# The low part of six weight halves moves from VectorE to GpSimd

## The chip, the cores and the metric

The kernel runs on one core of a Trainium2 chip. The metric is the time of one execution on the device in microseconds (us); less is better. The engines are called as the profile calls them: PE is TensorE's matrix multiplication, PEld its weight loads, DVE is VectorE, ACT is ScalarE, POOL is GpSimd, SP is SyncE, whose queue issues the weight loads from memory.

## The reference

Two layers of a hybrid decoder trunk over 256 positions of width 1024, in float32. A layer is a feed-forward block, a mixer block (causal pooling and block-sparse attention in parallel, merged by gates) and a second feed-forward block. The change touches the first block of the first layer only:

```python
def rms_norm(x, g):
    xf = x.astype(jnp.float32)
    y = xf * lax.rsqrt(jnp.mean(xf * xf, axis=-1, keepdims=True) + EPS)
    return (y * g.astype(jnp.float32)).astype(x.dtype)

def swiglu(h, w_gate_up, w_down):
    a, b = jnp.split(h @ w_gate_up, 2, axis=-1)
    return (jax.nn.silu(a) * b) @ w_down

def hybrid_layer(x, ...):
    x = x + 0.5 * swiglu(rms_norm(x, ffn1_norm), ffn1_w_gate_up, ffn1_w_down)
    ...
```

The hidden width of the block is 2816, which is 22 slices of 128.

## The kernel before, in words

**Split operands.** Each float32 operand is multiplied as two parts: a high part `hi` in a rounded format that TensorE multiplies fast, and a low part `lo`, which is the operand minus its high part. For weights ACT makes the high part with a copy (line 123) and DVE the low part with a subtraction (line 124). A product takes one multiplication of the weight's high part with both parts of the activations (512 columns) and one of its low part with the activations' high part (256 columns).

**Units.** Weights come in units of 128 x 2048 numbers (1 MB), in the order of use, `NU` of them. `request` (line 98) asks for the next one: it takes a buffer for the raw unit out of four, lets SP's queue load it, and splits each half (128 x 1024) into `hi` and `lo`; these have six buffers each, which is three units of two halves. `unit` hands the oldest unit that was asked for to the multiplications.

**The first feed-forward block.** One unit holds the weights of one slice of 128 hidden channels, gate and up side by side. `pair` (line 174) multiplies a unit by the activations into a PSUM tile `ps`, asks for the next unit, and drains the tile: ACT copies the half with the correction to SBUF (line 186), DVE adds the main half (line 187). PSUM has two such tiles, so unit n+2 cannot start before the drain of unit n is through. In the profile's rows the drained tiles are called `hold` for the first eight slices and `ab` after.

**The norm's factor comes late.** The multiplications start on activations that are not normalised, and the factor `r`, one number for each position, is applied to the drained tiles. It is made in `factor_spread`: the sum of squares is put through TensorE (`ss`), then ACT takes the reciprocal root (line 303) and DVE refines it (lines 302 and 304 to 306). Units 0 to 2 are worked side by side at the start; unit 3 follows with the sum of squares in its midst. Slices that were drained before `r` is there are finished afterwards, at most two for each further unit (lines 349 to 357): DVE multiplies by `r` (353), ACT takes the SiLU (355), DVE multiplies gate by up (356), and `halves` makes the two parts of the product (202 on ACT, 203 on DVE).

**Order of work.** Every engine works through its own queue in order. TensorE's order is that of the code. DVE's, ACT's and POOL's order is set when the program is built, by a scheduler that weighs what is ready; only operations marked `keep` stay in the order of the code. POOL has no work after the first 10 us in this kernel.

Of the kernel before, what the change touches and what calls it, by code (L numbers as in the profile page):

```python
# [18 lines left out]
F32 = mybir.dt.float32  # L19
F32R = mybir.dt.float32r  # L20
AF = mybir.ActivationFunctionType
OP = mybir.AluOpType
# [16 lines left out]
HALF = 8 * P  # L39
# [11 lines left out]
def trunk_kernel(ctx: ExitStack, tc: tile.TileContext, x_in, w_in, pw_in, qkn_in, rope_in, mask_in, band_in, out):  # L51
    nc = tc.nc
# [10 lines left out]
    def quarter(name):  # L63
        return pat.tile([P, 2, S], F32, name=name, tag="at")
# [11 lines left out]
    tt = nc.vector.tensor_tensor  # L76
# [6 lines left out]
    def banks(pool, name):  # L83

        return pool.tile([P, 2, 2, S], F32, name=name, tag="mm" if pool is pmm else "at2")
# [6 lines left out]
    def unit():  # L92

        if not ahead:
            request()
        return ahead.pop(0)

    def request(then=(), put=lambda i: i):

        if n_unit[0] == NU:  # L100
            return
        raw, hi, lo = buffers()
        u = n_unit[0]
        n_unit[0] += 1
        n = HALF if u < 4 else 2 * HALF
        for c in range(0, 2 * HALF, n):
            nc.sync.dma_start(raw[:, c:c + n], w_in[u, :, c:c + n])
        for h in range(2):
            split(raw[:, h * HALF:(h + 1) * HALF], hi[h], lo[h], put)
            for t, ps in then[h:h + 1]:  # L110
                drain(t, ps, put)
                for f in range(4 + 2 * h, 6 + 2 * h):
                    square_x(f, put)
        ahead.append((hi, lo))

    def buffers():
        raw = raws.tile([P, 2 * HALF], F32, name="raw", tag="raw")
        hi = [parts.tile([P, HALF], F32R, name="hi", tag="hi") for _ in range(2)]
        lo = [parts.tile([P, HALF], F32R, name="lo", tag="lo") for _ in range(2)]
        return raw, hi, lo  # L120

    def split(w, hi, lo, put=lambda i: i):
        put(act(hi, w, AF.Copy))  # L123
        put(tt(lo, w, hi.bitcast(F32), op=OP.subtract))  # L124

    def blk(z, b, n=1):

# [13 lines left out]
    def chain(ps, hi, lo, b, xk, first, last):  # L141

        prod(ps, blk(hi, b), xk, first, False)
        return prod(ps[:, 0, :], blk(lo, b), xk[:, 0, :], False, last)

    def chain3(ps, hi, lo, b, xs, first=True, last=True):

        for i, xk in enumerate(xs):
            prod(ps, blk(hi, b + i), xk[:, 0, :], first and i == 0, False)
            prod(ps, blk(hi, b + i), xk[:, 1, :], False, False)  # L150
            prod(ps, blk(lo, b + i), xk[:, 0, :], False, last and i == len(xs) - 1)

    def columns(w, ps, ks):

        for k in ks:
            for j in range(2):
                chain(ps[j] if isinstance(ps, list) else ps[:, j], *w, 2 * k + j, hk[k], k == 0, k == NK - 1)
# [13 lines left out]
            for k, j, d in bs:  # L171
                prod(d[:, 1, :], blk(hi, 2 * k + j), hk[k][:, 1, :], False, False)

    def pair(w, t, other=None, at=0, more=True):

        ps = banks(pmm, "ps")
        columns(w, ps, range(at))
        if other:
            other()
        columns(w, ps, range(at, NK))  # L180
        if more:
            request()
        drain(t, ps)

    def drain(t, ps, put=lambda i: i):
        put(act(t, ps[:, :, 1, :], AF.Copy))
        put(tt(t, ps[:, :, 0, :], t, op=OP.add))

    def pairs(ws, ts):

        pss = [banks(pmm, "ps"), banks(pmm, "ps"), [quarter("pe") for _ in range(2)]]
        for a, b in PIECES:
            for w, ps in zip(ws, pss):
                columns_high(w, ps, range(a, b), a == 0 and w is ws[0])
        request(list(zip(ts[:2], pss)), keep)
        for j, pe in enumerate(pss[2]):
            keep(act(ts[2][:, j, :], pe[:, 1, :], AF.Copy))
            keep(tt(ts[2][:, j, :], pe[:, 0, :], ts[2][:, j, :], op=OP.add))

    def halves(d, v, put=lambda i: i):  # L200

        put(act(d[:, 0, :], v, AF.Copy))
        put(tt(d[:, 1, :], v, d[:, 0, :].bitcast(F32), op=OP.subtract))
# [41 lines left out]
    def square_x(f, put=lambda i: i):  # L245

        if f == 0:
            act(acc, x[:, f, :], AF.Square)
        else:
            sq = small.tile([P, S], F32, name="sq", tag="sq", bufs=2)  # L250
            put(act(sq, x[:, f, :], AF.Square))
            put(tt(acc, acc, sq, op=OP.add))
# [38 lines left out]
    def factor_spread(mid=lambda: None, put=lambda i: i):  # L291


        ar = small.tile([P, 2, S], F32R, name="ar", tag="dr", bufs=1)
        halves(ar, acc, put)
        r = small.tile([P, S], F32, name="r", tag="r", bufs=2)
        h, a = (small.tile([P, S], F32, name=n, tag="sq", bufs=2) for n in "ha")
        ss = quarter("ss")[:, 0]
        for j in range(2):
            prod(ss, one_r, ar[:, j, :], j == 0, j == 1)  # L300
        mid()
        put(nc.vector.tensor_scalar(h, ss, 1.0 / D, EPS, op0=OP.mult, op1=OP.add))
        put(act(r, ss, AF.Abs_reciprocal_sqrt, scale=1.0 / D, bias=eps))
        stt(a, r, -0.5, r, op0=OP.mult, op1=OP.mult)
        tt(a, a, h, op=OP.mult)
        stt(r, a, 1.5, r, op0=OP.add, op1=OP.mult)
        return r

    def bc2(a):
        return a.unsqueeze(1).to_broadcast([P, 2, a.shape[-1]])  # L310

    def ffn(after, n0=0, end=False):
        gs = []
        for n, m in (("ga", 8), ("gc", 8), ("gb", NF - 16)):
            g = acts.tile([P, m, 2, S], F32R, name=n, tag=n)
            gs.extend(g[:, i] for i in range(m))
        abs_ = []

        hold = acts.tile([P, NK, 2, S], F32, name="hold", tag="gates")

        def wide():
            i = len(abs_)
            abs_.append((i, hold[:, i] if i < NK else tmp.tile([P, 2, S], F32, name="ab", tag="t512", bufs=5)))
            return abs_[-1][1]

        r = []

        def sums(*a):
            r.append(factor_spread(*a))

        if n0:
            pairs([unit() for _ in range(n0)], [wide() for _ in range(n0)])
            pair(unit(), wide(), lambda: sums(lambda: request((), keep), keep), 6, False)
        else:
            ws = [unit() for _ in range(2)]
            ts = [wide() for _ in range(2)]
            pss = [banks(pmm, "ps") for _ in range(2)]
            for u, k0, k1 in ((0, 0, NK - 1), (1, 0, 2), (0, NK - 1, NK), (1, 2, 4)):
                columns(ws[u], pss[u], range(k0, k1))
            drain(ts[0], pss[0])  # L340
            sums()
            columns(ws[1], pss[1], range(4, NK))
            drain(ts[1], pss[1])
        done = 0
        for i in range(n0 + 1 if n0 else 2, NF + 1):
            if i < NF:
                pair(unit(), wide())

            todo = range(done, min(done + 2, i) if i < NF else NF)
            done = todo.stop  # L350
            for j in todo:
                ab = abs_[j][1]
                tt(ab, ab, bc2(r[0]), op=OP.mult)
                sg = small.tile([P, S], F32, name="sg", tag="sg", bufs=2)
                act(sg, ab[:, 0, :], AF.Silu)
                tt(sg, sg, ab[:, 1, :], op=OP.mult)
                halves(gs[j], sg)
        for b in range(NK * NF):
            f, k = divmod(b, NF)
            if b % 16 == 0:  # L360
                hi, lo = unit()
            if k == 0:
                ps = quarter("ps")
            if f < NK - 1 or not end:
                chain(ps, hi, lo, b % 16, gs[k], k == 0, k == NF - 1)
            else:
                chain3(ps[:, 0, :], hi, lo, b % 16, gs[k:k + 1], k == 0, k == NF - 1)
            if k == NF - 1:
                add_x(f, ps, f < NK - 1 or not end)
                after(f)  # L370

    def add_x(f, ps, two):
        t = x[:, f, :]
        if two:
            t = small.tile([P, S], F32, name="t", tag="sg", bufs=2)
            act(t, ps[:, 1, :], AF.Copy)
            stt(t, t, 0.5, x[:, f, :], op0=OP.mult, op1=OP.add)
        keep(stt(x[:, f, :], ps[:, 0, :], 0.5, t, op0=OP.mult, op1=OP.add))  # L378
# [108 lines left out]
    def mix(l, after):  # L487
# [19 lines left out]
        def gate(f, *other):  # L507
            pair(unit(), gates[:, f], *other)
# [312 lines left out]
```

## Time and profile before

| | |
|---|---|
| median of 3 runs | 1007.2 us (1003.53, 1007.2, 1007.35) |
| the profiled execution | 1003.93 us |
| its span, first to last instruction | 1002.1 us |
| busy: PE, DVE, ACT, POOL | 997.7, 791.6, 623.0, 5.3 us |
| granted clock of TensorE | 1.0 |
| stretch 20 to 65 us: DVE, ACT, POOL busy | 43.05, 35.08, 0.00 of 45 us |

A row of the profile names a line of the kernel, an engine, an operation, what it writes and reads (`out<-in`, without buffer numbers), shapes and the number of instructions. In rows in order of time the first two numbers are start and duration in us, and brackets tell how long the engine stood idle before and who ended that. In rows of groups the numbers after the bar are busy time in us, the mean of one in ns, and idle time before. In rows of waits they are the total in us, how often, and the longest.

### The profile page before, as it was taken

How to read it: one execution, taken by the hardware profiler on the slowest of the kernel's cores; microseconds unless marked ns; L12 is line 12 of the kernel's file. 1: busy time of each engine (PE TensorE's matmuls, PEld its weight loads, DVE VectorE, ACT ScalarE, POOL GpSimd, SP SyncE). 2: the span in 40 equal slices, each digit the busy share in tenths (PEclk: the TensorE clock that was granted, in tenths of full speed). 3: DMA queues.
4: the chain of work that ended last, by engine and by line, in shares of the span. 5: the costliest groups of instructions: out<-in, count | busy, mean ns of one | idle time of the engine just before them, and what ended most of it. 6: DMA issues, size and time to landing. Idle time of an engine off the chain costs nothing.

```text
span 1002.1 us, 16021 instructions
## 1 busy us (share of the span) xinstructions
PE 997.7 (100%) x6350; PEld 906.2 (90%) x6350; DVE 791.6 (79%) x1168; ACT 623.0 (62%) x976; POOL 5.3 (1%) x34
## 2 busy tenths in 40 slices
PE   9999999999999999999999999999999999999998
PEld 8888899898999988988889999888989999888898
DVE  7998866599878888886688888666997888888752
ACT  7866655557756766665576666556678567666541
POOL 2000000000000000000000000000000000000000
PEclk9999999999999999999999999999999999999999
DMA  9676555643536665565556566555544365565640
GB/s 313 253 248 214 186 201 202 219 170 128 210 127 210 206 214 173 206 210 191 191 187 215 182 209 206 183 201 189 185 181 167 135 214 202 190 202 196 208 149 22
DMA packets 31163, 192.91 MB, mean 192 GB/s; under 512 B 3504, under 2 KB 7344, under 8 KB 8560
## 3 DMA queue, kind: packets, MB, share of 16 engines
q1 hardware_dynamic: 30528, 190.79, 55.5%
q8 instruction: 50, 0.82, 0.3%
q0 software_dynamic: 272, 0.79, 0.3%
q10 hardware_dynamic: 288, 0.31, 0.1%
q14 instruction: 25, 0.20, 0.1%
HBM read 190.82 MB, written 1.05 MB: 191 GB/s over the span
## 4 chain that ended last, share of the span: by engine, by line
PE 100%; DVE 0%; issue 0%
PE ps L81 85%; PE pt L81 6%; PE two L81 4%; PE at L81 2%; PE pe L81 1%; PE at L470 1%; PE busy L81 0%; PE tp L432 0%; PE st L81 0%; PE ss L81 0%; DVE gx L378 0%; DVE ones L212 0%; DVE eps L220 0%
## 5 line engine op out<-in xcount | busy, mean ns | idle before, releaser
L81 PE MATMUL ps<-hx,hi 128*128 128x512 f32 (+1 forms) x1714 | 572.8, 383 | 0.0
L124 DVE TENSOR_TENSOR lo<-raw,hi 128x1024 fp32r<-128x1024 f32 (+2 forms) x372 | 439.9, 1188 | 135.1 <-ACT hi L123 127.4
L123 ACT ACTIVATE hi<-raw 128x1024 fp32r<-128x1024 f32 (+2 forms) x372 | 380.2, 1030 | 230.4 <-PE ps L81 182.6
L81 PE MATMUL ps<-hx,lo 128*128 128x256 f32 x1712 | 464.6, 273 | 0.0
L81 PEld LDWEIGHTS ps<-hx,hi 128*128 128x128 f32 x1714 | 320.9, 188 | 57.2 <-issue 0.3
L81 PEld LDWEIGHTS ps<-hx,lo 128*128 128x128 f32 x1712 | 321.2, 188 | 0.9
L81 PE MATMUL ps<-gc,hi 128*128 128x512 f32 (+1 forms) x264 | 87.0, 376 | 0.0
L81 PE MATMUL ps<-ga,hi 128*128 128x512 f32 (+1 forms) x264 | 87.0, 376 | 0.0
L81 PE MATMUL ps<-gc,lo 128*128 128x256 f32 x256 | 69.9, 273 | 0.0
L81 PE MATMUL ps<-ga,lo 128*128 128x256 f32 x256 | 69.9, 273 | 0.0
L81 PE MATMUL ps<-gb,hi 128*128 128x512 f32 (+1 forms) x198 | 65.6, 376 | 0.0
L81 PE MATMUL pt<-hi,hx 128*128 128x512 f32 x192 | 65.1, 385 | 0.0
L81 PEld LDWEIGHTS ps<-ga,hi 128*128 128x128 f32 x264 | 49.0, 188 | 8.3
L81 PEld LDWEIGHTS ps<-gc,hi 128*128 128x128 f32 x264 | 49.0, 188 | 8.3
L81 PE MATMUL pt<-lo,hx 128*128 128x256 f32 x192 | 52.6, 274 | 0.0
L81 PE MATMUL ps<-gb,lo 128*128 128x256 f32 x192 | 52.4, 273 | 0.0
L81 PEld LDWEIGHTS ps<-ga,lo 128*128 128x128 f32 x256 | 48.1, 188 | 0.0
L81 PEld LDWEIGHTS ps<-gc,lo 128*128 128x128 f32 x256 | 48.1, 188 | 0.0
L81 PE MATMUL ps<-mk,hi 128*128 128x256 f32 x256 | 44.1, 275 | 0.0
L81 PE MATMUL two<-yp,hi 128*128 128x256 f32 x256 | 44.1, 275 | 0.0
L81 PEld LDWEIGHTS ps<-gb,hi 128*128 128x128 f32 x198 | 36.7, 188 | 6.2
L81 PEld LDWEIGHTS pt<-hi,hx 128*128 128x128 f32 x192 | 36.0, 188 | 6.8
(149 smaller groups left out, 1041.4 us busy)
## 6 DMA issues: line engine op xcount, KB each, us to landing
raw<-w SPq DMA_DIRECT2D x176, 1024.0 KB, 4.9
raw<-w SPq DMA_DIRECT2D x18, 128.0 KB, 4.0
raw<-w SPq DMA_DIRECT2D x2, 512.0 KB, 6.8
out_dram<-gx SPq DMA_DIRECT2D x8, 128.0 KB, 1.9
raw<-w SPq DMA_DIRECT2D x3, 256.0 KB, 5.2
gx<-x POOLq DMA_DIRECT2D x4, 128.0 KB, 4.6
qk<-pw SPq DMA_DIRECT2D x2, 256.0 KB, 2.7
gx<-x POOLq DMA_DIRECT2D x1, 256.0 KB, 4.3
```

The lines of the kernel that those rows point to most:

```text
L81: return keep(nc.tensor.matmul(*args, **kw))
L123: put(act(hi, w, AF.Copy))
L124: put(tt(lo, w, hi.bitcast(F32), op=OP.subtract))
L470: keep(nc.tensor.transpose(pt[:, h, o * P:(o + 1) * P], pr[:, h, c * P:(c + 1) * P], ident))
```

## The change

`split` gets a parameter for the engine that makes the low part, and `request` and `pair` hand it down. In the first block of the first layer (`n0` is 3 there and 0 elsewhere) the six calls of `pair` with `i` from 4 to 9 ask for their units with GpSimd; `request` uses it for the second half of a unit only. So six instructions of 128 x 1024 move from DVE to POOL: the second low part of units 5 to 10. Everything else of the code stays.

```diff
-    def request(then=(), put=lambda i: i):
+    def request(then=(), put=lambda i: i, low=nc.vector.tensor_tensor):
...
-            split(raw[:, h * HALF:(h + 1) * HALF], hi[h], lo[h], put)
+            split(raw[:, h * HALF:(h + 1) * HALF], hi[h], lo[h], put, low if h else tt)
...
-    def split(w, hi, lo, put=lambda i: i):
+    def split(w, hi, lo, put=lambda i: i, low=tt):
         put(act(hi, w, AF.Copy))
-        put(tt(lo, w, hi.bitcast(F32), op=OP.subtract))
+        put(low(lo, w, hi.bitcast(F32), op=OP.subtract))
...
-    def pair(w, t, other=None, at=0, more=True):
+    def pair(w, t, other=None, at=0, more=True, low=tt):
...
         if more:
-            request()
+            request(low=low)
         drain(t, ps)
...
             if i < NF:
-                pair(unit(), wide())
+                pair(unit(), wide(), low=nc.gpsimd.tensor_tensor if n0 and i < 10 else tt)
```

The scheduler also orders the rest of DVE's work anew. From the second step of the norm's factor, DVE's rows before (`lo_469` and `lo_470` are the low parts of unit 5, `lo_526` and `lo_527` of unit 6, `lo_583` and `lo_584` of unit 7; `ps_374` and `ps_433` are the PSUM tiles of units 3 and 4):

```order
L304 SCALAR_TENSOR_TENSOR a_404<-r_402 128x256
L187 TENSOR_TENSOR hold_240<-ps_374,hold_240 128x512
L305 TENSOR_TENSOR a_404<-a_404,h_403 128x256
L124 TENSOR_TENSOR lo_470<-raw_466,hi_468 128x1024
L306 SCALAR_TENSOR_TENSOR r_402<-a_404,r_402 128x256
L124 TENSOR_TENSOR lo_526<-raw_523,hi_524 128x1024
L353 TENSOR_TENSOR hold_240<-hold_240,r_402 128x512 x2
L124 TENSOR_TENSOR lo_527<-raw_523,hi_525 128x1024
L187 TENSOR_TENSOR hold_240<-ps_433,hold_240 128x512
L353 TENSOR_TENSOR hold_240<-hold_240,r_402 128x512
```

and now, from the same instruction:

```order
L304 SCALAR_TENSOR_TENSOR a_404<-r_402 128x256
L187 TENSOR_TENSOR hold_240<-ps_374,hold_240 128x512
L305 TENSOR_TENSOR a_404<-a_404,h_403 128x256
L124 TENSOR_TENSOR lo_526<-raw_523,hi_524 128x1024
L306 SCALAR_TENSOR_TENSOR r_402<-a_404,r_402 128x256
L124 TENSOR_TENSOR lo_583<-raw_580,hi_581 128x1024
L353 TENSOR_TENSOR hold_240<-hold_240,r_402 128x512 x3
L187 TENSOR_TENSOR hold_240<-ps_433,hold_240 128x512
L353 TENSOR_TENSOR hold_240<-hold_240,r_402 128x512 x2
```

Ahead of the drain of unit 4 (`ps_433`), two L124 are gone, the first low part of unit 7 has moved in, and a third L353 stands there.

POOL's queue now, from its last transfer of the start on; before, the first of these rows was followed by the last two at once:

```order
L708 DMA gx_79<-x 128x512
L124 TENSOR_TENSOR lo_470<-raw_466,hi_468 128x1024
L124 TENSOR_TENSOR lo_527<-raw_523,hi_525 128x1024
L124 TENSOR_TENSOR lo_584<-raw_580,hi_582 128x1024
L124 TENSOR_TENSOR lo_641<-raw_637,hi_639 128x1024
L124 TENSOR_TENSOR lo_693<-raw_689,hi_691 128x1024
L124 TENSOR_TENSOR lo_745<-raw_741,hi_743 128x1024
L816 UNCONDITIONAL_BRANCH
L816 ISA
```

Each of the six waits for ACT's high part and for TensorE's release of its buffer, and TensorE waits for POOL at the middle of units 5 to 10.

## The prediction

> **What bounds the kernel now.** I read the page's busy times and its chain first. The chain is the path that set the end, followed back from the last instruction.
>
> ```profile
> PE 997.7 (100%) x6350; PEld 906.2 (90%) x6350; DVE 791.6 (79%) x1168; ACT 623.0 (62%) x976; POOL 5.3 (1%) x34
> PE 100%; DVE 0%; issue 0%
> ```
>
> TensorE is the whole chain, so the change can only win time in which TensorE waits, and it loses whatever it makes TensorE wait. Matmul ends are modelled, so the waits are best read at the weight loads (PEld): first all of them over the run, then a table of stretches of 5 us.
>
> ```profile
> PEld ps L81 <- DVE hold L187: 0.3, 1, 0.3
> PEld ps L81 <- DVE ab L187: 0.2, 1, 0.2
> 35.00:40.00 5.00, 4.96 (x30) 4.20 (x29) 5.00 (x9) 4.33 (x8) 0.00 (x0) 1.00 0.86 251
> 45.00:50.00 5.00, 5.00 (x32) 4.50 (x31) 5.00 (x9) 3.66 (x8) 0.00 (x0) 1.00 0.46 185
> 60.00:65.00 5.00, 5.00 (x31) 4.34 (x30) 4.97 (x7) 2.97 (x5) 0.00 (x0) 1.00 0.96 349
> 38.67 0.19 PEld L81 LDWEIGHTS ps<-hx,hi 128*128 128x128 f32 x1 [0.34 <-DVE hold L187]
> 60.25 0.19 PEld L81 LDWEIGHTS ps<-hx,hi 128*128 128x128 f32 x1 [0.19 <-DVE ab L187]
> ```
>
> Columns of the stretches after the bounds: length, then busy time of PE, PEld, DVE, ACT, POOL, then clock and DMA. Full pace is 4.50 of PEld in 5 us (45 to 50). Only two stretches fall short, each by one wait for L187, the addition that frees a PSUM pair: at 38.67 for unit 6 (it takes the pair of unit 4) and at 60.25 for unit 10. Together 0.34 + 0.19 = 0.5 us. From unit 6 to unit 10 it is 60.25 - 38.67 = 21.58 us, less the 0.19: 5.35 us a unit at full pace. VectorE (DVE) is busy through these stretches (5.00, 5.00, 4.97 of 5.00): it has work waiting, TensorE almost never.
>
> **What the change can win.** It takes six L124 off DVE. These rows are DVE's order of work after the first norm's sum:
>
> ```profile
> 29.20 1.22 DVE L124 TENSOR_TENSOR lo<-raw,hi 128x1024 fp32r<-128x1024 f32 x1
> 31.70 0.42 DVE L304 SCALAR_TENSOR_TENSOR a<-r 128x256 f32<-128x256 f32 x1 [1.29 <-ACT r L303]
> 32.05 0.68 DVE L187 TENSOR_TENSOR hold<-ps,hold 128x512 f32<-128x512 f32 x1
> 32.65 0.41 DVE L305 TENSOR_TENSOR a<-a,h 128x256 f32<-128x256 f32 x1
> 34.12 0.42 DVE L306 SCALAR_TENSOR_TENSOR r<-a,r 128x256 f32<-128x256 f32 x1
> 34.45 1.22 DVE L124 TENSOR_TENSOR lo<-raw,hi 128x1024 fp32r<-128x1024 f32 x1
> 35.59 1.29 DVE L353 TENSOR_TENSOR hold<-hold,r 128x512 f32<-128x512 f32 x2
> 36.79 1.22 DVE L124 TENSOR_TENSOR lo<-raw,hi 128x1024 fp32r<-128x1024 f32 x1
> 37.93 0.68 DVE L187 TENSOR_TENSOR hold<-ps,hold 128x512 f32<-128x512 f32 x1
> 39.13 0.75 DVE L356 TENSOR_TENSOR sg<-sg,hold 128x256 f32<-128x256 f32 x2
> 41.54 0.75 DVE L203 TENSOR_TENSOR ga<-sg,ga 128x256 fp32r<-128x256 f32 x2
> 42.21 1.22 DVE L124 TENSOR_TENSOR lo<-raw,hi 128x1024 fp32r<-128x1024 f32 x1
> 25.52 3.89 ACT L123 ACTIVATE hi<-raw 128x1024 fp32r<-128x1024 f32 x4
> 31.57 3.89 ACT L123 ACTIVATE hi<-raw 128x1024 fp32r<-128x1024 f32 x4
> ```
>
> From start to start an L124 takes 35.59 - 34.45 = 1.14 us, an L353 half of 1.20 (0.60), an L356 or L203 half of 0.67 (0.34; 42.21 - 41.54). L187 is taken at 0.60, like the L353 of its size. The change frees 6 x 1.14 = 6.8 us of DVE. With nothing in the way, the drain of unit 4 moves up: the L124 of unit 7 needs the third of the high parts begun at 31.57 (about 34.5), it and three L353 take 1.14 + 1.80, and L187 starts at 37.44, before 37.93. Unit 6 could start at 38.67 - 0.34 = 38.33 and no longer waits. So the gain ends at 0.5 us: TensorE has no more to give, and the rest of the 6.8 us becomes idle DVE.
>
> **What it can lose: the price on GpSimd.** No row shows a two-input operation there. The nearest are its fills, of 1, 64 and 128 columns:
>
> ```profile
> L233 POOL MEMSET inv<- 128x1 f32 x8 | 0.3, 98 | 0.0
> L227 POOL MEMSET uT<- 128x64 f32 x1 | 0.2, 152 | 0.0
> masks.py:197 POOL MEMSET ident<- 128x128 f32 x1 | 0.2, 204 | 0.3 <-POOLq L810 0.3
> 5.07 1.08 DVE L124 TENSOR_TENSOR lo<-raw,hi 128x256 fp32r<-128x256 f32 x3
> ```
>
> The fills grow by (204 - 98) / 127 = 0.83 ns a column, 0.85 us for 1024. If two reads and one write overlap, one L124 there is 0.1 + 0.85 = 0.95 us; if the three go one after the other, 0.1 + 3 x 0.85 = 2.6 us. On DVE the same operation is 0.34 us at 256 columns (three from 5.07 to the next DVE row at 6.07, below) and 1.14 at 1024, 1.04 ns a column with both inputs read at once; read in turn that is 2 x 1.04 x 1024 + 0.1 = 2.2 us. I take 2.2, since this row is the same operation on the same tiles, and keep 0.95 and 2.6. [...]
>
> Taken alone, 2.2 us on an idle engine costs nothing. Each of these parts is wanted when its unit is half done, for unit 5 at 38.33 - 5.35 / 2 = 35.7, and its high part is ready at 25.52 + 3.89 = 29.41. Behind these instructions POOL's queue holds only the end of the program.
>
> **What it can lose: GpSimd and DVE at once.** Before, the two engines overlap in three places:
>
> ```profile
> 4.68 0.18 POOL L704 COPY pace<-hx 128x1 f32<-128x1 f32 x1 [2.68 <-ACT hx L242]
> 6.13 0.46 POOL L704 COPY pace<-hx 128x1 f32<-128x1 f32 x1
> 9.26 0.43 POOL L704 COPY pace<-hx 128x1 f32<-128x1 f32 x1 [1.60 <-ACT hx L242]
> 4.65 0.49 DVE L243 SCALAR_TENSOR_TENSOR hx<-gx,hx 128x256 fp32r<-128x256 f32 x1 [0.37 <-ACT hx L242]
> 6.07 0.47 DVE L243 SCALAR_TENSOR_TENSOR hx<-gx,hx 128x256 fp32r<-128x256 f32 x1
> 9.16 0.48 DVE L243 SCALAR_TENSOR_TENSOR hx<-gx,hx 128x256 fp32r<-128x256 f32 x1 [1.18 <-ACT hx L242]
> ```
>
> The copy moves one column. Begun 0.03 us after DVE's two-input operation it takes 0.18. Begun 0.06 and 0.10 after it takes 0.46 and 0.43, and ends at 6.59 and 9.69, 0.05 behind DVE's 6.54 and 9.64 both times. That is what one operation held until the other is through looks like. [...]
>
> [...] If a POOL L124 holds DVE for 2.2 us, each removed 1.14 costs 2.2 in its place. What that does to the drains depends on who is served first when both are ready, so I work both out.
>
> *GpSimd first.* Unit 5's part waits for the L124 begun at 29.20 and runs 30.4 to 32.6: L304 goes from 31.70 to 32.6, and L187 of unit 3 follows. Unit 6's part (high part ready about 33.5) runs 33.5 to 35.7 and holds L305. Unit 7's (ready 35.46) runs 36.05 to 38.25. Only then come L124 1.14, L306 0.34, L124 1.14, three L353 1.80: L187 of unit 4 starts at 42.67, ends 0.68 later, and unit 6 starts at about 43.4, not 38.33: 5.1 us of waiting, less the 0.5 that goes: +4.6. Later drains keep up: L187 of unit 5 comes after 0.60 + 1.20 + 0.67 + 1.14 + 0.67, with a small wait for ACT at about 47.2, and ends before unit 7 wants it at 48.8.
>
> *GpSimd last.* Unit 5's part still runs 30.4 to 32.6, since DVE waits for L303 then (+0.9). The rest goes in only under drains or where DVE waits. L187 of unit 4 starts at 37.44 + 0.87 = 38.3 and unit 6 waits 0.6. Unit 6's part starts with it and holds DVE until 40.5; 1.20 + 0.67 + 1.14 bring 43.5; unit 7's part runs there to 45.7, two L203 follow, and L187 of unit 5 starts at 46.35: unit 7, due at 44.3, waits 2.7. Unit 8 waits 0.8 the same way, the later ones 0.2 together: 4.3, less 0.5: +3.8.
>
> The mean is +4.2. At 1.8 us a part the same steps give +2.1 to +3.4, at 2.6 +5.9 to +6.5, at 0.95 about +0.3 to +1.2. ACT's order shifts too, but it waits on DVE here, and SP's loads wait for the low parts with a unit to spare, so neither gets a price of its own.
>
> **The sum.** The profiled execution took 1003.93 us, 1.8 around its span of 1002.1. With +4.2 it would take 1008.1. The three runs have their median at 1007.20, 3.3 above the profiled one, and the change is added to that: 1007.2 + 4.2 = 1011.4.
>
> **Rivals.**
> - *Slower: GpSimd's part takes over 2.4 us and holds DVE.* The place is the drains of units 4 to 9. From 2.4 the sum passes 5 us: +5 at 2.4, +6.2 at the upper bound of 2.6, 1013.4. For it: 2.6 is in reach by the fill rows, and six hand-overs may each cost a little. Against it: that needs reads and writes not to overlap at all.
> - *No hold:* DVE runs as if alone. For it: the copy at 4.68. Against it: the other two. Then only the 0.5 us goes: 1006.7.
> - *DVE always wins, GpSimd starves:* DVE loses nothing, and the part comes late itself. Unit 5's gets 30.4 to 31.7 and the drain at 32.05, 1.9 of 2.2 us, and ends under the next drain near 37.8; TensorE wanted it at 35.9, 0.2 after the unit's middle. That is 1.9, and some 0.5 for each of the next three units: 3.4 - 0.5 = +2.9, 1010.1. For it: both late copies were the ones held.
>
> **Chances.** Forecast (hold, up to 2.4 us) 0.42; longer than that 0.34; starving 0.11; no hold 0.13. A measurement of this kernel tells about 0.5%, 5 us, from no change (three runs of one kernel span 3.8 us). Forecast, starving and no hold lie within 5 us; the rival of the long part does not. With the scatter between runs: slower 0.35, same 0.62, faster 0.03, for nothing in the trace holds 5 us to win. The likeliest case alone spans 1.8 to 2.4 us a part, 1009.3 to 1012.7. The range reaches down past the case of no hold, since the median may fall nearer the fastest run of 1003.53, and up past 2.6 us a part: 1004.5 to 1014.0.
>
> **What the new profile would show.** Six POOL rows of L124 at 2.0 to 2.4 us each; L304 starting about 0.9 later than 31.70; DVE rows of L353, L305 or L356 lengthened, or idle ahead of them, while POOL runs; PEld waits for L187 of some 4 to 5 us, the first at unit 6 or 7; PEld short of 4.50 between 35 and 50, and a span near 1006. I am wrong if DVE's rows beside POOL's keep 0.68 and 0.42 us and start on time (no hold), if TensorE waits for the low part from POOL rather than for L187 (starving), or if POOL's rows are far from 2.2.

## The result and the profile after

| | before | after |
|---|---|---|
| median of 7 runs each, taken on one chip | 1003.88 us (1003.37 to 1007.35) | 1011.11 us (1009.95 to 1014.51) |
| the profiled execution and its span | 1003.93, 1002.1 us | 1011.11, 1009.1 us |

The ratio of after to before is 1.0064 with a 95 % interval from 1.0049 to 1.0079. (Ratios here and below are not the quotients of the two medians, and can differ a little from them.) By the ratio the changed kernel is 6.4 us slower, by the medians 7.2; the two profiled spans differ by 7.0 us.

The page of the kernel after: busy times of the engines, the granted clock of TensorE in 40 equal slices, and the chain of work that ended last by engine.

```profile
PE 1000.0 (99%) x6350; PEld 908.1 (90%) x6350; DVE 795.0 (79%) x1162; ACT 623.2 (62%) x976; POOL 21.6 (2%) x40
PEclk9899999999999999999999999999999999999999
PE 95%; DMA 1%; ACT 1%; DVE 1%; issue 0%; SPq 0%; ACTq 0%; DVEq 0%
```

Three things are to be seen. DVE has six instructions less (1162 against 1168) and is busy 3.4 us longer. The clock has one low slice, the second, which runs from 25 to 50 us. And the chain, which was TensorE alone, now passes through other engines. The weight loads after 33 us say where TensorE stands still; these are groups of waits (what waits, for whom: us in total, how often, the longest).

```profile
PEld ps L81 <- DVE hold L187: 4.4, 1, 4.4
PEld ps L81 <- ACT hi L123: 0.6, 1, 0.6
```

Now the same place in order of time: weight loads of the kernel after at unit 5 (33.52), at the end of unit 5 (38.64) and at unit 6.

```profile
33.52 0.19 PEld L81 LDWEIGHTS ps<-hx,hi 128*128 128x128 f32 x1 [0.57 <-ACT hi L123]
...
38.64 0.19 PEld L81 LDWEIGHTS ps<-hx,lo 128*128 128x128 f32 x1
43.19 0.29 PEld L81 LDWEIGHTS ps<-hx,hi 128*128 128x128 f32 x1 [4.36 <-DVE hold L187]
...
48.48 0.33 PEld L81 LDWEIGHTS ps<-hx,lo 128*128 128x128 f32 x1
48.87 0.19 PEld L81 LDWEIGHTS ps<-hx,hi 128*128 128x128 f32 x1
```

Unit 6 waits 4.36 us for L187, and then its loads take 0.33 us each, not 0.19, until 48.87. From 43.19 to 48.87 there are nine pairs of `hi` and `lo`, 0.64 us a pair once it runs evenly. At full pace a pair takes 0.335 us (5.35 us for the 16 of a unit), so the nine would have taken 3.01 us: 5.68 - 3.01 = 2.67 us are lost after the wait is over. The clock says why; in these stretches of the kernel after, the columns are length, busy time of PE, PEld, DVE, ACT and POOL, then clock and DMA.

```profile
35.00:40.00 5.00, 4.14 (x26) 3.47 (x24) 5.00 (x3) 2.08 (x3) 4.31 (x2) 1.00 0.76 264
40.00:45.00 5.00, 1.81 (x5) 1.60 (x6) 5.00 (x10) 2.07 (x4) 0.00 (x0) 0.70 0.86 318
45.00:50.00 5.00, 5.00 (x21) 4.29 (x20) 4.90 (x8) 3.14 (x8) 2.56 (x1) 0.62 0.00 0
50.00:55.00 5.00, 5.00 (x32) 4.50 (x31) 4.44 (x7) 4.41 (x8) 2.38 (x1) 1.00 0.66 210
...
41.50:42.00 0.50, 0.00 (x0) 0.00 (x0) 0.50 (x2) 0.32 (x2) 0.00 (x0) 0.99 1.31 197
42.00:42.50 0.50, 0.00 (x0) 0.00 (x0) 0.50 (x2) 0.50 (x2) 0.00 (x0) 0.50 0.18 49
48.50:49.00 0.50, 0.50 (x4) 0.44 (x4) 0.50 (x1) 0.00 (x0) 0.50 (x1) 0.68 0.00 0
```

PE is "busy" for 5.00 of 5.00 us from 45 to 50 and does 21 multiplications there, not 32: busy time does not show a slow clock, the count and the clock column do. The clock falls to half at 41.99: a mean of 0.99 over the half microsecond before 42.00 leaves 0.01 us of it at half. It returns at 48.82: a mean of 0.68 from 48.50 is 0.32 us at half and 0.18 at full. That is 6.83 us at half clock, of which TensorE stood still until 43.19.

The account from this trace: 4.36 and 0.57 us of new waits, 2.67 us at half clock, less the 0.53 us of waits that went, are 7.1 us; the spans differ by 7.0.

Next, what held L187. POOL's rows of the kernel after, up to the fifth of its six subtractions, and then DVE's rows.

```profile
29.34 3.18 POOL L124 TENSOR_TENSOR lo<-raw,hi 128x1024 fp32r<-128x1024 f32 x1 [18.98 <-ACT hi L123]
33.50 5.82 POOL L124 TENSOR_TENSOR lo<-raw,hi 128x1024 fp32r<-128x1024 f32 x2 [0.97 <-ACT hi L123]
46.48 2.56 POOL L124 TENSOR_TENSOR lo<-raw,hi 128x1024 fp32r<-128x1024 f32 x1 [7.17 <-ACT hi L123]
52.62 2.38 POOL L124 TENSOR_TENSOR lo<-raw,hi 128x1024 fp32r<-128x1024 f32 x1 [3.57 <-ACT hi L123]
```

```profile
31.56 1.25 DVE L304 SCALAR_TENSOR_TENSOR a<-r 128x256 f32<-128x256 f32 x1 [1.28 <-ACT r L303]
32.73 0.68 DVE L187 TENSOR_TENSOR hold<-ps,hold 128x512 f32<-128x512 f32 x1
33.33 0.41 DVE L305 TENSOR_TENSOR a<-a,h 128x256 f32<-128x256 f32 x1
33.66 3.42 DVE L124 TENSOR_TENSOR lo<-raw,hi 128x1024 fp32r<-128x1024 f32 x1
37.00 2.60 DVE L306 SCALAR_TENSOR_TENSOR r<-a,r 128x256 f32<-128x256 f32 x1
39.52 1.21 DVE L124 TENSOR_TENSOR lo<-raw,hi 128x1024 fp32r<-128x1024 f32 x1
40.65 1.88 DVE L353 TENSOR_TENSOR hold<-hold,r 128x512 f32<-128x512 f32 x3
42.46 0.68 DVE L187 TENSOR_TENSOR hold<-ps,hold 128x512 f32<-128x512 f32 x1
...
46.06 0.75 DVE L203 TENSOR_TENSOR ga<-sg,ga 128x256 fp32r<-128x256 f32 x2
46.92 0.69 DVE L187 TENSOR_TENSOR hold<-ps,hold 128x512 f32<-128x512 f32 x1
```

L304 took 0.42 us before and takes 1.25 beside POOL's first part. The L124 begun at 33.66 takes 3.42 in place of 1.22, L306 2.60 in place of 0.42. Here the two engines take turns: part, L124, part, L306, each waiting for the end of the other's operation. POOL's rows hold such waits too: the one of 46.48 began while the second L203 was still at work, until 46.81, and the rest of it is 2.23 us. L187, which reads one tile in PSUM and one in SBUF, keeps its 0.69 us in the middle of that row. After L306 come L124 and three L353, and only then L187 of unit 4, which frees the PSUM pair for unit 6.

The wait of 0.57 us at unit 5 comes from the first part in the same way, though its row names ACT's L123. The high parts of unit 5 had been ready since 29.26. Unit 5 takes the PSUM pair of unit 3, whose L187 stands behind the held L304; it ends at 33.41, and unit 5 starts 0.11 us later. In a run further down (units 5 to 7 with work in the wait) the distance is 0.11 us too, and there the row of the multiplication names L187.

### The profile page after: what moved, and what is told of

Same layout as the page of the kernel before. It is cut to its first block, busy times and chain, and to the rows that moved or that the text cites. A ratio compares the mean times of both kernels' runs of the same rounds, so it can differ in the third digit from the quotient of the medians.

```text
span 1009.1 us, 16033 instructions
## 1 busy us (share of the span) xinstructions
PE 1000.0 (99%) x6350; PEld 908.1 (90%) x6350; DVE 795.0 (79%) x1162; ACT 623.2 (62%) x976; POOL 21.6 (2%) x40
## 4 chain that ended last, share of the span: by engine, by line
PE 95%; DMA 1%; ACT 1%; DVE 1%; issue 0%; SPq 0%; ACTq 0%; DVEq 0%
PE ps L81 82%; PE pt L81 6%; PE two L81 4%; PE at L81 2%; DMA raw<-w 1%; ACT hi L123 1%; PE at L470 1%; PE tp L432 0%; DMA gx<-x 0%; SPq L712 0%; DVE r L306 0%; DVE hold L353 0%; ACT hold L186 0%; PE st L81 0%; DVE hold L187 0%
## 5 line engine op out<-in xcount | busy, mean ns | idle before, releaser
L124 DVE TENSOR_TENSOR lo<-raw,hi 128x1024 fp32r<-128x1024 f32 (+2 forms) x366 | 435.2, 1195 | 137.1 <-ACT hi L123 129.2
L123 ACT ACTIVATE hi<-raw 128x1024 fp32r<-128x1024 f32 (+2 forms) x372 | 379.9, 1030 | 235.5 <-PE ps L81 187.6
```

What stands on the lines that cost most here:

```text
L124: put(low(lo, w, hi.bitcast(F32), op=OP.subtract))
```

## The experiments

Two theories stood against each other at first: the time goes because GpSimd and DVE hold each other ahead of one drain (then the parts of units 5 to 7 carry the loss), or every part costs its share. When the clock had been seen, a second question came: does the half clock cost time of its own, or would TensorE only have waited for DVE somewhere else?

### How many parts, and which

**Units 5 to 7 alone.**

```diff
-  low=nc.gpsimd.tensor_tensor if n0 and i < 10 else tt
+  low=nc.gpsimd.tensor_tensor if n0 and i < 7 else tt
```

> Only the low parts of units 5, 6 and 7 go to GpSimd. Theory (hold and clock): the changed kernel loses its time ahead of the drain of unit 4, where the parts of units 5 to 7 hold VectorE, and by the half clock that follows that wait of 4.4 us. Then three parts cost what six do: one PEld wait for L187 at unit 6 of about 4.4 us, a stretch of some 5 us at a granted clock near 0.5, in all +7 us against the kernel before (ratio 1.006 to 1.008). Rival (every part costs the same wherever it stands): half, +3.5 us, ratio 1.0035.

Measured: 1011.11 us median against 1004.35 of before on that chip, ratio 1.0078 (1.0050 to 1.0105), the time of all six parts. The profiled execution was the slowest of its six (1020.13; the others 1010.0 to 1011.7) and lost time after 50 us, so only its rows before that are read: the wait at unit 6, and the clock behind it.

```profile
43.73 0.29 PEld L81 LDWEIGHTS ps<-hx,hi 128*128 128x128 f32 x1 [4.35 <-DVE hold L187]
...
45.00:50.00 5.00, 5.00 (x20) 4.29 (x19) 5.00 (x10) 3.75 (x7) 0.00 (x0) 0.60 0.21 52
```

So in the change the whole loss comes with the parts of units 5 to 7.

**Units 8 to 10 alone.**

```diff
-  low=nc.gpsimd.tensor_tensor if n0 and i < 10 else tt
+  low=nc.gpsimd.tensor_tensor if n0 and 7 <= i < 10 else tt
```

> Only the low parts of units 8, 9 and 10 go to GpSimd; VectorE's order up to the drain of unit 4 is that of the kernel before. Theory (hold): the parts still hold VectorE for 2.3 us each while it has its backlog; by the same steps as in the forecast that gives waits of some 2.4 us at unit 7 and 1.9 us at unit 9, and none at unit 6: +4 us. If the clock only falls after a long wait, it stays at 1.00 here and the total is +4 us (ratio 1.004); if any wait for the drain brings it down, +7 us or more. Rival (the loss belongs to the first three parts alone): no more than 0.5 us either way.

Measured: 1007.89 us, ratio 1.0032 (1.0020 to 1.0043), +3.5 us. These are its two longest waits for L187 at the weight loads, and the rows of POOL and DVE that meet.

```profile
56.02 0.19 PEld L81 LDWEIGHTS ps<-hx,hi 128*128 128x128 f32 x1 [0.72 <-DVE hold L187]
62.98 0.19 PEld L81 LDWEIGHTS ps<-hx,hi 128*128 128x128 f32 x1 [1.66 <-DVE ab L187]
...
50.17 9.68 POOL L124 TENSOR_TENSOR lo<-raw,hi 128x1024 fp32r<-128x1024 f32 x2 [4.45 <-ACT hi L123]
...
57.54 3.40 DVE L124 TENSOR_TENSOR lo<-raw,hi 128x1024 fp32r<-128x1024 f32 x1
```

Alone, the later parts cost something too, since DVE's backlog is still there when they meet it. The size was about as expected, but the waits are shorter and stand elsewhere: 0.52, 0.72 and 1.66 us at units 8, 9 and 10, where 2.4 us at unit 7 and 1.9 us at unit 9 had been expected. The clock stays at 1.00. In the change itself these parts cost nothing that can be told, presumably because TensorE has been put back by then. The costs of parts do not add up: ratios of 1.0078 and 1.0032 for the halves, 1.0064 for all six.

The two engines don't take turns here. Of the two parts in POOL's row the first alone takes 6.90 us: from 50.53 to 54.82 seven two-input operations of DVE run ahead of it, and it gets through in 2.25 us once DVE stands idle ahead of L187. The part before it takes 4.29 us in the same way, until DVE comes to L187. Why DVE goes ahead here, and the parts of units 6 and 7 were served in turn in the change, no run tells.

**Units 5 and 6.**

```diff
-  low=nc.gpsimd.tensor_tensor if n0 and i < 10 else tt
+  low=nc.gpsimd.tensor_tensor if n0 and i < 6 else tt
```

> Only units 5 and 6 on GpSimd. Theory (each part ahead of the drain of unit 4 holds VectorE for one more 2.3 us): wait for L187 at unit 6 of about 2.9 us minus what the order gives, and 0.8 us at unit 9; +3.4 us without a loss of clock. If a wait of this length is enough for the half clock, 2.7 us more: +6 us. Rival (all or nothing with three parts): no wait at unit 6 above 0.5 us.

Measured: 1008.00 us against 1004.83, ratio 1.0027 (1.0014 to 1.0041). The wait at unit 6, and the two stretches in which the clock falls and comes back:

```profile
42.50 0.19 PEld L81 LDWEIGHTS ps<-hx,hi 128*128 128x128 f32 x1 [2.12 <-DVE hold L187]
...
43.00:43.50 0.50, 0.50 (x3) 0.40 (x3) 0.50 (x2) 0.00 (x0) 0.00 (x0) 0.53 0.00 0
46.00:46.50 0.50, 0.50 (x4) 0.42 (x3) 0.50 (x2) 0.50 (x2) 0.00 (x0) 0.56 0.27 115
```

Without the part of unit 7, L306 is not held (0.41 us), and the wait is 2.24 us shorter than in the change. Here the clock is low from 43.03 to 46.44, for 3.41 us, and begins to be so 0.53 us after TensorE has resumed. Not every execution shows it: of the twelve, five have a mean clock of 0.998, one of 0.999 and six of 1.000.

**Unit 5 alone.**

```diff
-  low=nc.gpsimd.tensor_tensor if n0 and i < 10 else tt
+  low=nc.gpsimd.tensor_tensor if n0 and i < 5 else tt
```

> Only unit 5 on GpSimd. Theory: L304 is held from 31.7 to about 32.6 us, the wait at unit 6 is about 0.7 us and one of about 0.7 us at unit 9: +1.1 us (ratio 1.001), clock 1.00. Rival (no cost while VectorE waits for ScalarE anyway): as before or 0.3 us less.

Measured: 1005.53 us against 1004.83, ratio 0.9997 (0.9981 to 1.0013): no difference that can be told, where some 1 us was expected; the interval reaches to 1.3. The hold itself is there: L304 beside POOL, and the wait of unit 5, which again starts 0.11 us behind the end of L187 of unit 3 (34.35).

```profile
32.50 1.25 DVE L304 SCALAR_TENSOR_TENSOR a<-r 128x256 f32<-128x256 f32 x1 [1.29 <-ACT r L303]
34.46 0.19 PEld L81 LDWEIGHTS ps<-hx,hi 128*128 128x128 f32 x1 [0.58 <-ACT hi L123]
```

### What holds DVE

**GpSimd writes, but reads nothing.** Three fills take the place of each subtraction.

```diff
+    def fills(lo, w, hi, op):
+        for _ in range(2):
+            nc.gpsimd.memset(lo.bitcast(F32), 0.0)
+        return nc.gpsimd.memset(lo.bitcast(F32), 0.0)
...
-  low=nc.gpsimd.tensor_tensor if n0 and i < 10 else tt
+  low=fills if n0 and i < 10 else tt
```

> GpSimd does not read: each of the six subtractions is replaced by three fills of the same tile with zeros, about 0.9 us each by the slope of the fills, 2.6 us together, so the six low parts are left out of the result. VectorE's order around the drain of unit 4 is that of the change. Theory (a GpSimd operation that reads SBUF holds VectorE's two-input operations): L304, L124 and L306 keep 0.42 and 1.22 us, no PEld wait for L187 above 0.3 us, clock 1.00, time as before or up to 0.5 us less. Rival (it is the new order, or that the low parts come late from GpSimd): a wait of some 4 us at unit 6 and +7 us as in the change.

Measured: 1004.74 us against 1004.35, ratio 0.9996 (0.9986 to 1.0006). The lines of this kernel stand five further down (L306 is L311). Two of POOL's rows and one of DVE's that lies within them:

```profile
34.28 1.98 POOL L124 MEMSET lo<- 128x1024 f32 x2 [2.37 <-PE ps L81]
36.31 0.95 POOL L125 MEMSET lo<- 128x1024 f32 x1
...
35.02 0.42 DVE L311 SCALAR_TENSOR_TENSOR r<-a,r 128x256 f32<-128x256 f32 x1
```

GpSimd is at work for 2.9 us per part, longer than the 2.23 to 2.34 us of a subtraction alone, and DVE's L306 keeps its 0.42 us, where it took 2.60 in the change. So here the work on GpSimd and its writes did not hold DVE; the subtraction, which reads SBUF as well, did. The run shows a second thing: here DVE is rid of the six L124 and is not held, and the time is that of before. The most that this move could have brought is nothing measurable.

**GpSimd reads one tile in place of two.** A copy takes the place of each subtraction.

```diff
+    def copies(lo, w, hi, op):
+        return nc.gpsimd.tensor_copy(lo, w)
...
-  low=nc.gpsimd.tensor_tensor if n0 and i < 10 else tt
+  low=copies if n0 and i < 10 else tt
```

> GpSimd reads one tile instead of two: each of the six subtractions is replaced by a copy of the raw weights into the low part, about 1 us each by the slope of the fills, so the six low parts are wrong in the result. Theory (any GpSimd operation that reads SBUF holds VectorE's two-input operations): rows of L304, L124, L306, L353 or L356 that meet a copy are longer by up to 1 us, each copy that meets one is longer too, but there are fewer us of it: +0 to +1.5 us. Rival (only two inputs on both sides meet): VectorE's rows keep 0.42, 0.68 and 1.22 us.

Measured in a single execution: 1004.11 us against a median of 1004.83. Its lines stand three further down; a POOL row and the DVE row that meets it:

```profile
33.65 1.68 POOL L123 CAST lo<-raw 128x1024 fp32r<-128x1024 f32 x1 [2.72 <-PE ps L81]
...
34.35 1.27 DVE L309 SCALAR_TENSOR_TENSOR r<-a,r 128x256 f32<-128x256 f32 x1
```

L306 is held again, to 1.27 us: it ends at 35.62, 0.29 us behind the copy. In this run one input in SBUF was enough on GpSimd's side. But the copy is short, 1.10 us in the shortest of the six rows, so the holds last about as long as the L124 that left DVE (1.22 us), and this one execution took no longer than before. This suggests that the length of the operation on GpSimd counts against that of the one it replaces.

### What the half clock costs

**Work for TensorE in the wait, all six parts.** 18 multiplications into a spare quarter of PSUM stand ahead of unit 6.

```diff
+            if n0 and i == 6:
+                fill = quarter("fill")
+                for _ in range(18):
+                    prod(fill, one_r, hk[0], True, True)
```

> The changed kernel with 18 multiplications of 128 x 512 more on TensorE between units 5 and 6, into a PSUM tile that nobody reads: some 4 us of work in the wait of 4.4 us, so TensorE has something to do there. Theory (the clock falls because TensorE stands still): the granted clock stays at 1.00 from 40 to 50 us, the 2.7 us of slow multiplications go, unit 6 starts when it did, and the kernel takes some 4.4 us more than before instead of 7 (ratio 1.0044, about 2.7 us faster than the change). Rival (the clock falls for another reason, GpSimd and VectorE at work together): clock near 0.5 again and +7 us.

Measured: 1011.46 us, ratio 1.0071 (1.0055 to 1.0086), no better than the change. Its waits, and the stretch in which the clock had been low:

```profile
43.28 0.19 PEld L81 LDWEIGHTS ps<-hx,hi 128*128 128x128 f32 x1 [0.39 <-DVE hold L187]
55.56 0.19 PEld L81 LDWEIGHTS ps<-hx,hi 128*128 128x128 f32 x1 [1.64 <-DVE hold L187]
67.09 0.19 PEld L81 LDWEIGHTS ps<-hx,hi 128*128 128x128 f32 x1 [0.90 <-DVE ab L187]
...
40.00:45.00 5.00, 5.00 (x25) 3.98 (x24) 5.00 (x9) 1.99 (x4) 0.00 (x0) 1.00 0.88 321
```

The clock stays at 1.00 and unit 6 begins at 43.28, as in the change. The 2.67 us are not saved, though: TensorE now waits 1.64 and 0.90 us for later drains. Either it meets at full pace the work that DVE is behind with, or the added lines have reordered DVE's queue: one L356 and two L203 that followed the drain of unit 6 now stand ahead of it. This run cannot tell the two apart.

**The same with units 5 to 7 alone** (both edits above).

> Units 5, 6 and 7 on GpSimd, and the 18 multiplications that keep TensorE busy in the wait before unit 6. Behind unit 7 no GpSimd part holds VectorE any more, so its backlog is not fed. Theory (the half clock is worth 2.7 us by itself): clock 1.00 from 40 to 50 us, no later wait for L187 above 0.7 us, +4.5 us in all (ratio 1.0045), about 2.6 us less than with the first three parts alone (1.0078). Rival (VectorE's backlog sets the time, and the slow clock only stands where the next waits would): later waits of 2 us or more take its place as in the fill of the whole change, +7 us again.

Measured: 1010.79 us against 1004.83, ratio 1.0058 (1.0037 to 1.0079); clock 1.00, and again a late wait:

```profile
56.45 0.19 PEld L81 LDWEIGHTS ps<-hx,hi 128*128 128x128 f32 x1 [1.66 <-DVE hold L187]
```

The order of DVE's queue had moved here as well. A clean test needs a wait where DVE has no backlog and the order stays.

**A wait made on purpose, in the kernel before.** Ahead of unit 14 TensorE does one small multiplication of a tile that GpSimd fills k times; k sets the wait. At that place DVE has time to spare (in the control it is busy for 4.02 to 4.34 of each 5 us from 80 to 95). The control has k = 1, the others 7, 7 with 18 multiplications in the wait, and 5.

```diff
+            if n0 and i == 14:
+                sc = uT[:, :, PAD:]
+                nc.gpsimd.tensor_copy(sc[:, 0, :1], abs_[12][1][:, 0, :1])
+                for _ in range(1):
+                    nc.gpsimd.memset(sc, 0.0)
+                fill = quarter("fill")
+                mm(fill[:, 0, :P], lhsT=ones, rhs=sc[:, 0, :P], start=True, stop=True)
```

The control:

> Control for the next three. The kernel before, all low parts on VectorE, with a small multiplication on TensorE between units 13 and 14 that reads a tile which GpSimd fills: one fill of about 1 us that begins when unit 12 is drained, so it is through before TensorE gets there. At this place VectorE has no backlog. Every theory expects the time of the kernel before within 0.5 us.

Measured: 1004.70 us against 1005.29, ratio 0.9986 (0.9971 to 1.0001); no wait, clock 1.00.

k = 7:

> As the control, but with seven fills in a row, about 7 us, so that TensorE waits some 4.3 us between units 13 and 14 for GpSimd alone; GpSimd only writes, and VectorE isn't held. Theory (a wait of this length brings the granted clock to a half, and that costs some 2.7 us of its own): +7 us, and a stretch of about 5 us at a clock near 0.5 right behind the wait. Rival (the slow clock needs VectorE and GpSimd at work against each other, or costs nothing that the wait has not cost already): +4.3 us.

k = 7 with `for _ in range(18): prod(fill, one_r, hk[0], True, True)` ahead of the last line:

> The same wait, with 18 multiplications of 128 x 512 ahead of the one that waits, 4 us of work into a tile that nobody reads. The order of VectorE's and ScalarE's work is that of the run with the wait alone, which the fill between units 5 and 6 of the change did not keep. Theory (standing still lowers the clock): clock 1.00 throughout, +4.3 us, 2.7 us less than the wait alone. Rival: as the wait alone.

k = 5:

> As the wait alone with five fills instead of seven: TensorE waits some 2.3 us. [...] Rival (any wait brings the full loss): +5 us.

Measured: 1012.31, 1010.64 and 1011.10 us; ratios 1.0066 (1.0048 to 1.0085), 1.0049 (1.0033 to 1.0066) and 1.0053 (1.0035 to 1.0070). Against the control that is +7.6, +5.9 and +6.4 us. The wait and the stretch behind it, for k = 7:

```profile
88.80 0.50 PEld L81 LDWEIGHTS fill<-uT,ones 128*128 128x128 f32 x2 [6.17 <-POOL uT L350]
90.00:95.00 5.00, 5.00 (x26) 4.40 (x25) 0.46 (x1) 1.06 (x1) 0.00 (x0) 0.79 0.00 0
```

with the multiplications in the wait:

```profile
88.06 0.30 PEld L81 LDWEIGHTS fill<-uT,ones 128*128 128x128 f32 x2 [2.24 <-POOL uT L350]
85.00:90.00 5.00, 3.19 (x18) 2.48 (x17) 1.57 (x4) 0.83 (x2) 2.86 (x3) 1.00 0.64 218
```

and for k = 5:

```profile
86.96 0.50 PEld L81 LDWEIGHTS fill<-uT,ones 128*128 128x128 f32 x2 [4.13 <-POOL uT L350]
90.00:95.00 5.00, 5.00 (x23) 4.40 (x22) 1.20 (x1) 1.06 (x1) 0.00 (x0) 0.71 0.00 0
```

With k = 7, five pairs of loads at 0.64 us follow the wait, 1.5 us lost; 6.17 + 1.5 = 7.7, measured 7.6. Filled with work, the same wait leaves the clock at 1.00 and the kernel is 1.7 us faster, though it does 18 multiplications more. With k = 5, nine slow pairs follow, 2.67 us lost as in the change; 4.13 + 2.67 = 6.8, measured 6.4 (6.7 between the two profiled spans). So at this place the half clock came with TensorE standing still and cost time of its own, and the wait of 4.13 us cost more of it (2.67 us) than the one of 6.17 (1.5 us). The waits were longer than expected, 4.13 where 2.3 us had been worked out; the loss is read against the wait that occurred. From which length on a wait brings the clock down, no run tells: behind 1.66 us it stayed at 1.00 (units 8 to 10 alone), behind 2.12 it was at half for 3.41 us (units 5 and 6).

## Why the prediction was right or wrong

The time, 1011.11 us, lies 0.3 under the forecast of 1011.4, and that is partly luck. The forecast stood on a base of 1007.2 us, where seven runs now give 1003.88, and added 4.2, where the spans now differ by 7.0. Both steps were off by about 3 us, in opposite directions. The likeliest outcome, "same" (within 0.5 %), had 0.62; what came is "slower", which had 0.35, by a ratio of 0.64 % (0.49 to 0.79, so only just).

1. *What bounds the kernel; a gain of at most 0.5 us.* Right. The run with fills frees DVE without any hold and reads 0.9996.
2. *The price of a part, 2.2 us.* Right. POOL's rows are longer, 2.38 us and more, but each of them began beside a two-input operation of DVE. From the end of that operation to its own end each of the six took 2.23 to 2.34 us. The rival of the long part, over 2.4 us, has a time, +5 to +6.2, that is nearer to the measured one, but its mechanism isn't what made the difference: waits of 4.36 + 0.57 us are no more than the 5.1 that the forecast had at 2.2 us a part.
3. *The hold.* Right. Before, two copies of one column (0.46 and 0.43 us beside DVE, 0.18 for the third) were all that spoke for it. In the change the rows of 3.42 and 2.60 us, 1.22 and 0.42 before, agree that the later of the two operations waited for the end of the other, and the run with fills agrees that a GpSimd operation without a read left DVE alone (L306 0.42 us). The row of 6.90 us with units 8 to 10 does not agree: DVE's operations that began after that part ran ahead of it. The steps of the forecast also let L187 pass beside a part of GpSimd, while its neighbours in DVE's queue are held; no run before shows that. In the change the L187 of 46.92 kept 0.69 us beside a part, and the two L356 behind it took 2.13 us, where two take 0.75.
4. *Who is served first.* Of the two orders worked out, "GpSimd first" is nearly what came: L187 of unit 4 was put at 42.67 and unit 6 at 43.4; they are at 42.46 and 43.19. In detail they alternate: L305 went ahead of unit 6's part, not behind it, and one L124 between the parts of units 6 and 7, not behind both. "GpSimd last" is what it was averaged with; in the change that order did not occur, and no wait of 2.7 us at unit 7 with it. The rival in which GpSimd starves did not occur there either, but two of the three parts did starve when units 8 to 10 were moved alone.
5. *The sum.* This is the step that failed, and by a term left out, not by one of the wrong size. New waits less the old ones are 4.36 + 0.57 - 0.53 = 4.4 us, against 4.2 predicted. The sum took a wait of TensorE to cost its own length. It cost 2.67 us more, since TensorE came out of it at half clock. Before, the clock stood at 1.00 in every stretch quoted, and I took it as given.
6. *Costs put at nothing.* Loads on SP's queue: right, ACT never waits for a raw unit between 22 and 70 us. ACT's order: right too, up to unit 6 it is that of before. The 0.57 us at unit 5 come from the late L187 of unit 3. The forecast had that drain late, ending at 33.6 by its own steps where unit 5 was due at 38.33 - 5.35 = 33.0, but drew no wait from it; the total is the same, since the drain of unit 4 sets the start of unit 6.

What stays open: whether the change without the slow clock would be 2.67 us faster. With work in the wait its place was taken by later waits, but DVE's order had changed too. That the half clock costs time of its own is shown only where DVE has no backlog (1.7 us between the wait of k = 7 and the same wait with work in it). Executions of one kernel that differ in their mean clock point the same way for the change, but they are few, and hardly any has a trace: with units 5 and 6, six executions at 1.000 have a median span of 1005.5 us and five at 0.998 one of 1006.2; for the change itself see the last section.

## What to carry to other kernels

Before moving an operation of DVE to GpSimd, ask whether both will read SBUF at the same time: then what counts is how long DVE is held (here 2.60 us for an L306 of 0.42), against the operation that it is rid of (1.22 us), and which drain stands in DVE's queue behind the held ones. Where TensorE is the bound, a new wait of some microseconds may not be priced by its length alone (here 2.67 us came on top of 4.36): look at the clock column behind it, and count instructions, since busy time hid the slow clock (5.00 of 5 us with 21 multiplications in place of 32). When one cause has been found, make the account of the whole difference; here the wait explained 4.4 of 7.0 us, and only the remainder pointed to the clock.

## What the runs showed of the hardware

**The half clock lasted 6.8 us, and 3.41 us in one run.** From the means of the 5 us stretches, 0.70 and 0.62 in the change, 0.72 and 0.60 with units 5 to 7, 0.53 and 0.79 for k = 7, 0.61 and 0.71 for k = 5: what is missing to 1.00 is 0.68 both together each time, which is 0.68 x 5 / 0.5 = 6.8 us at half. With units 5 and 6 it was 3.41 us, half of that. There TensorE had loaded weights until 40.37 and again from 42.50, and the clock fell at 43.03, 0.53 us after TensorE was back at work. What sets these lengths and the moment of the fall, no run tells.

**The price was not set by the length of the wait.** Time is lost in the part of the half clock in which TensorE has work: 2.67 us behind waits of 4.36 and 4.13 us, 1.5 us behind 6.17, nothing behind 1.66 with units 8 to 10 alone and behind 2.24 with work ahead of it (clock 1.00 in both). Behind 2.12 the clock was at half for 3.41 us in the profiled execution, and not at all, by the mean clock of 1.000, in six of the other eleven. In the change itself three of seven executions have a mean clock of 0.996 and spans of 1009.1 to 1009.5 us, the profiled one among them; four have 0.998, and three of these have spans of 1007.9 to 1008.1, some 1.3 us less (the fourth took 1012.5). By the clock, with 0.002 missing to 1.000 in place of 0.004, these would have been at half for about half as long, an estimate; no trace of one was taken.

**A copy of one column took 1.11 us beside a subtraction.** The made-up wait for k = 7 began with it; POOL's row, and the row of DVE that it met.

```profile
80.56 1.11 POOL L348 COPY uT<-ab 128x1 f32<-128x1 f32 x1 [69.71 <-DVE ab L360]
...
80.42 1.22 DVE L124 TENSOR_TENSOR lo<-raw,hi 128x1024 fp32r<-128x1024 f32 x1
```

It begins 0.14 us after the subtraction and ends at 81.67, 0.03 behind it.
